# Turning the projections of a one-layer decoder round: activations stationary, 512 weight columns moving

## The chip, the cores and the metric

The kernel runs on one NeuronCore of a Trainium2 chip. The metric is the device time of one execution in microseconds, the median of several runs. A NeuronCore has a matrix engine (TensorE, "PE" in the profile; its weight loads are "PEld"), a vector engine (DVE), a scalar engine (ACT), GpSimd (POOL) and a queue engine that issues most DMAs (SP). A matrix product loads a stationary operand of 128 x 128 into the array and then streams a moving operand of up to 512 columns through it; the result goes into a PSUM bank of 512 floats per partition.

## The reference

One layer of a decoder trunk for 256 tokens of width 2048, in float32. Every `@` below is a projection with float32 weights:

```python
def swiglu(h, w_gate, w_up, w_down):
    return (jax.nn.silu(h @ w_gate) * (h @ w_up)) @ w_down      # d_ff = 5632
...
h = rms_norm(x, ffn1_norm[l])
x = x + 0.5 * swiglu(h, ffn1_w_gate[l], ffn1_w_up[l], ffn1_w_down[l])
h = rms_norm(x, mix_norm[l])
z = h @ w_in[l]
b_g, c_g, u, q_nsa, kv_nsa, g_nsa, q_mem, g_merge = jnp.split(z, split_at, axis=-1)
y_conv = short_conv_mixer(b_g, c_g, u, conv_w[l])
y_nsa = nsa_attention(q_nsa, kv_nsa, g_nsa, ...)
y_mem = memory_cross_attention(q_mem, rms_norm(mem, mem_norm[l]), w_mem_kv[l], ...)
ys = jnp.stack([y_conv, y_nsa, y_mem], axis=2)
yb = jnp.einsum('bsnc,ncd->bsnd', ys, w_branch[l])
merged = jnp.einsum('bsnd,bsnd->bsd', jax.nn.sigmoid(g_merge...), yb)
x = x + merged @ w_o[l]
x = x + 0.5 * swiglu(rms_norm(x, ffn2_norm[l]), ...)
```

## The kernel before, in words

The weights are cut into tiles of 128 x 128. There are 6736 of them in the projections: 256 for the memory's keys and values (`w_mem`), 2112 in each feed-forward network (`w_ffn1`, `w_ffn2`), 2256 between them (`w_mix`). They are stored in HBM in the order of their use and come in chunks of eight (512 KB) through `Stream.fetch`: one DMA, an ACT copy that rounds the chunk to the short float format fp32r (`whi`), and a DVE subtraction that gives the rest (`wlo`). Each activation is likewise held as two parts, high and low, and a product is the sum of three: high times high, low times high and high times low. Four buffers each of `wraw`, `whi` and `wlo` let ACT and DVE run ahead of PE.

Activations lie feature-major: 128 features on the partitions, 256 tokens along the row. `proj` takes a group of two weight tiles columns at a time and walks over the 16 slices of the inner dimension. For each weight tile it issues two matrix products with the weight tile stationary: `whi` against 512 columns (the high and the low part of the 256 tokens side by side, L232) and `wlo` against the 256 columns of the high part (L233). Such a couple is called a pair below; 768 columns stream in it. The two halves of a bank then have to be added: `evac` copies one half with ACT (L243) and adds the other with DVE (L244). The per-token factor of the RMS norm is applied by a DVE multiplication with a row `rb` that holds it for all partitions.

The work of the attention is written as generators. `proj` calls `tick` at a few places of a group, which takes each running generator one step on, so that scores, transposes and softmax stand between projection products on PE's queue, which runs in order. A scheduler then arranges the instructions of each engine. `compress` (attention's block compression, L546 and L553) builds its input by four small DMAs on POOL's queue, adds the position code on DVE (`Rk`, `Rv`) and runs 64 records of products 60 columns wide on PE (float32 products appear in the trace as two records each, transposes as one). Sums over features are products with a column of ones (L336, L347, 2 columns wide); transposes are products with the identity (L301, L357, L393, L507, L523 in the projections' service, L482, L637, L681 in the attention).

Of the kernel before, what the change touches and what calls it, by code (L numbers as in the profile page):

```python
# [10 lines left out]
F32 = mybir.dt.float32  # L11
# [6 lines left out]
P = 128  # L18
# [4 lines left out]
NQ = 4  # L23
HPQ = HID // NQ
# [8 lines left out]
def order(group, late):  # L33


    out = []
    if late == "k":
        n = len(group[0])
        out = [(j, kts[i], i == 0, i == n - 1) for i in range(n) for j, kts in enumerate(group)]
    elif late:  # L40
        for j, kts in enumerate(group):
            out += [(j, k, i == 0, False) for i, k in enumerate(kts[:len(kts) - late])]
        for j, kts in enumerate(group):
            rest = kts[len(kts) - late:]
            out += [(j, k, False, i == late - 1) for i, k in enumerate(rest)]
    else:
        for j, kts in enumerate(group):
            out += [(j, k, i == 0, i == len(kts) - 1) for i, k in enumerate(kts)]
    return out
# [4 lines left out]

def plan_mem():
    gs = [([("kv", f, ALLK) for f in range(4)], "k")]
    return gs + [([("kv", 2 * p, ALLK), ("kv", 2 * p + 1, ALLK)], 0) for p in range(2, 8)]


def plan_ffn():  # L60
    gs = []
    for q in range(NQ):
        for f in range(q * HPQ, (q + 1) * HPQ):
            gs.append(([("gate", f, ALLK), ("up", f, ALLK)], 2 if f == 0 else 0))
        ks = list(range(q * HPQ, (q + 1) * HPQ))
        for p in range(8):
            gs.append(([("down", 2 * p, ks), ("down", 2 * p + 1, ks)], 1 if p == 0 else 0))
    return gs


def plan_mix():
    gs = []
    for p in range(4):
        gs.append(([("qm", 2 * p, ALLK), ("qm", 2 * p + 1, ALLK)], 2 if p == 0 else 0))
    for i in range(0, 8, 2):
        gs.append(([("c", i, ALLK), ("u", i, ALLK)], 0))
        gs.append(([("c", i + 1, ALLK), ("u", i + 1, ALLK)], 0))
        gs.append(([("b", i, ALLK), ("b", i + 1, ALLK)], 0))
    for n in (0, 2, 4, None, 1, 3, 5):
        gs.append(([("ng", 0, ALLK)] if n is None else [("nkv", 2 * n, ALLK), ("nkv", 2 * n + 1, ALLK)], 0))  # L80
    for p in range(4):
        gs.append(([("nq", 2 * p, ALLK), ("nq", 2 * p + 1, ALLK)], 0))
    for br in (0, 2, 1):
        for d in range(KT):
            gs.append(([("gm%d" % br, d, ALLK), ("wb%d" % br, d, list(range(8)))], 0))
    for p in range(8):
        gs.append(([("wo", 2 * p, ALLK), ("wo", 2 * p + 1, ALLK)], 2 if p == 0 else 0))
    return gs
# [11 lines left out]
RAMP = (2, 2, 4)  # L100


def tiles_of(plan):
    return [(g[j][0], g[j][1], k) for g, late in plan for j, k, _, _ in order([m[2] for m in g], late)]
# [14 lines left out]
class Stream:  # L119
# [13 lines left out]

    def fetch(self):
# [11 lines left out]

class Trunk:
    def __init__(self, ctx, tc, a):
# [3 lines left out]
        self.xs = pool("xs", bufs=16)  # L152
        self.hp = pool("hp", bufs=16)
# [14 lines left out]
        z = self.tp.tile([P, 2, 512], BF16, name="zero", tag="t", bufs=3)  # L168
# [44 lines left out]
    def proj(self, stream, group, late, X, ticks=0, before=None, fold=False):  # L213


        nc = self.nc
        pw = self.psw.tile([P, 2, 512], F32, name="psw", tag="psw")
        pss = [pw[:, 0, :], pw[:, 1, :]]
        pss += [self.psa.tile([P, 512], F32, name="pso", tag=tag) for tag in ("sc", "o")[:max(0, len(group) - 2)]]
        seq = order([m[2] for m in group], late)  # L220
        at = [len(seq) * (n + 1) // ticks - 1 for n in range(ticks)]
        for n, (j, k, first, last) in enumerate(seq):
            if before:
                before(j, k)
            wh, wl = stream.next((group[j][0], group[j][1], k))
            x = X[j][k]
            ps = pss[j]
            if fold:
                for n2 in range(2):
                    nc.tensor.matmul(ps[:, :S], wh, x[:, n2, :], start=first and n2 == 0, stop=False)  # L230
            else:
# [4 lines left out]
        return [pw] + pss[2:]  # L236

    def evac(self, ps, t=None, part=slice(0, 2)):
        nc = self.nc
        ps = ps[0]  # L240
        if t is None:
            t = self.tp.tile([P, 2, S], F32, name="t", tag="t", bufs=3)
        nc.scalar.activation(t[:, part], ps[:, part, S:], AF.Copy)  # L243
        nc.vector.tensor_tensor(t[:, part], ps[:, part, :S], t[:, part], op=ALU.add)  # L244
        return t

    def split(self, src, pool=None, tag="h", scale=None):

        nc = self.nc
        h = (pool or self.hp).tile([P, 2, S], F32R, name=tag, tag=tag)  # L250
# [718 lines left out]
```

## Time and profile before

| | |
|---|---|
| time, median of 3 runs | 2486.95 us (2474.59 to 2487.94) |
| the profiled execution | 2491.16 us; its span on the core 2489.4 us |
| PE busy | 2476.5 us, 99% of the span, 14388 records |
| PEld (weight loads) | 2153.6 us, 14388: one for each product |
| DVE busy | 1591.1 us, 64% |
| ACT busy | 1206.1 us, 48% |
| POOL busy | 32.8 us, 1% |
| HBM traffic | 460 MB, mean 185 GB/s |

The span is the time from the first to the last instruction of the core. Products on PE are pipelined, so the length that the profile gives for one (397 ns for 512 columns) is longer than the time from its start to the start of the next; what a product costs in a row of products is read from the starts.

### The profile page before, as it was taken

Reading aid. Unit: us, or ns where it says so; the run is one execution under the profiler, and the core shown is the slowest. Engines: PE = TensorE matmul, PEld = TensorE weight load, DVE = VectorE, ACT = ScalarE, POOL = GpSimd, SP = SyncE. Lnnn points to the kernel's source line nnn. Section 1 sums busy time; section 2 is a strip of 40 time slices with the busy share of each in tenths; the row PEclk is TensorE's granted clock in tenths of the full one; section 3 lists DMA queues with packets and bytes.
Section 4 is the critical chain, followed back from the end, with each engine's and each line's share of the span. In section 5 each row is a group of like instructions: output and inputs, shape, how many; then the busy total and the mean of one; then the engine's idle time right before and its main releaser. Section 6 shows DMA issues by size and latency. Waiting matters only on the chain.

```text
span 2489.4 us, 36404 instructions
## 1 busy us (share of the span) xinstructions
PE 2476.5 (99%) x14388; PEld 2153.6 (87%) x14388; DVE 1591.1 (64%) x2190; ACT 1206.1 (48%) x1660; POOL 32.8 (1%) x42
## 2 busy tenths in 40 slices
PE   9999999999999999999999999999999999999999
PEld 7888888888888888888888888888888888888888
DVE  8666566566566766744677776666666666666665
ACT  7544444444445544433455554555544444444443
POOL 0000000000000000010000000000000000000000
PEclk9999999999999999999999999999999999999999
DMA  7666666665666754654545546666666666666665
GB/s 269 180 186 187 187 187 186 186 187 186 187 186 195 237 168 153 187 177 157 166 153 155 157 154 184 189 190 207 187 190 189 192 187 193 188 189 191 190 190 161
DMA packets 128348, 459.98 MB, mean 185 GB/s; under 512 B 14512, under 2 KB 15024, under 8 KB 127664
## 3 DMA queue, kind: packets, MB, share of 16 engines
q1 hardware_dynamic: 127152, 454.50, 58.9%
q0 software_dynamic: 1024, 3.14, 0.4%
q8 instruction: 113, 1.85, 0.3%
q14 instruction: 59, 0.48, 0.0%
HBM read 452.35 MB, written 4.19 MB: 183 GB/s over the span
## 4 chain that ended last, share of the span: by engine, by line
PE 98%; DMA 1%; DVE 0%; POOL 0%; ACT 0%; SPq 0%; issue 0%; DVEq 0%; ACTq 0%
PE psw L232 62%; PE psw L233 32%; PE phid L553 1%; PE sc L652 1%; PE pt L681 0%; PE on L688 0%; PE sc L464 0%; DMA wraw<-w_mem 0%; PE pso L232 0%; PE o L489 0%; DMA Ek<-t 0%; DMA Ev<-t 0%; PE psw L230 0%; PE pstat L347 0%; PE on L702 0%; PE scc L615 0%
## 5 line engine op out<-in xcount | busy, mean ns | idle before, releaser
L232 PE MATMUL psw<-xs,whi 128*128 128x512 f32 x4432 | 1567.0, 397 | 0.0
L144 DVE TENSOR_TENSOR wlo<-wraw,whi 128x1024 fp32r<-128x1024 f32 (+1 forms) x844 | 1031.4, 1223 | 766.9 <-ACT whi L143 764.9
L143 ACT ACTIVATE whi<-wraw 128x1024 fp32r<-128x1024 f32 (+1 forms) x844 | 892.2, 1057 | 1043.2 <-PE psw L232 654.5
L233 PE MATMUL psw<-xs,wlo 128*128 128x256 f32 x4432 | 1245.8, 281 | 0.0
L232 PEld LDWEIGHTS psw<-xs,whi 128*128 128x128 f32 x4432 | 834.0, 188 | 199.3 <-issue 5.2
L233 PEld LDWEIGHTS psw<-xs,wlo 128*128 128x128 f32 x4432 | 840.1, 190 | 0.1
L232 PE MATMUL psw<-h,whi 128*128 128x512 f32 x2122 | 747.8, 396 | 3.0 <-ACT whi L143 3.0
L233 PE MATMUL psw<-h,wlo 128*128 128x256 f32 x2144 | 601.8, 281 | 0.0
L232 PEld LDWEIGHTS psw<-h,whi 128*128 128x128 f32 x2122 | 398.3, 188 | 95.9 <-ACT whi L143 4.1
L233 PEld LDWEIGHTS psw<-h,wlo 128*128 128x128 f32 x2144 | 405.6, 189 | 0.7 <-DVE wlo L144 0.6
L244 DVE TENSOR_TENSOR t<-psw,t 128x512 f32<-128x512 f32 x233 | 159.1, 683 | 8.9 <-ACT t L243 8.8
L243 ACT ACTIVATE t<-psw 128x512 f32<-128x512 f32 x233 | 135.7, 582 | 27.3 <-PE psw L233 26.9
L252 ACT ACTIVATE h<-s 128x256 fp32r<-128x256 f32 x88 | 36.9, 419 | 114.1 <-DVE s L371 114.1
L253 DVE TENSOR_TENSOR h<-s,h 128x256 fp32r<-128x256 f32 x88 | 37.4, 425 | 42.2 <-ACT h L252 42.2
L368 DVE TENSOR_TENSOR t<-t,rb 128x512 f32<-128x512 f32 x88 | 60.9, 692 | 3.1
L232 PE MATMUL psw<-yn,whi 128*128 128x512 f32 x128 | 45.7, 395 | 0.0
L378 DVE SCALAR_TENSOR_TENSOR x<-t,x 128x512 f32<-128x512 f32 x63 | 43.6, 692 | 2.2
L667 ACT ACTIVATE L<-L,nb 128x128 f32<-128x128 f32 x64 | 28.6, 447 | 32.2 <-DVE nb L665 32.2
L371 DVE TENSOR_TENSOR s<-s,t 128x256 f32<-128x256 f32 x88 | 36.9, 419 | 1.0 <-ACT s L370 1.0
L233 PE MATMUL psw<-yn,wlo 128*128 128x256 f32 x128 | 36.0, 282 | 0.0
L370 ACT ACTIVATE s<-t 128x256 f32<-128x256 f32 x88 | 35.3, 402 | 0.0
L232 PEld LDWEIGHTS psw<-yn,whi 128*128 128x128 f32 x128 | 24.1, 188 | 5.7
(185 smaller groups left out, 742.8 us busy)
## 6 DMA issues: line engine op xcount, KB each, us to landing
wraw<-w_ffn SPq DMA_DIRECT2D x528, 512.0 KB, 3.6
wraw<-w_mix SPq DMA_DIRECT2D x282, 512.0 KB, 3.6
wraw<-w_mem SPq DMA_DIRECT2D x31, 512.0 KB, 4.7
xin<-memT SPq DMA_DIRECT2D x8, 256.0 KB, 5.1
x<-xT SPq DMA_DIRECT2D x8, 256.0 KB, 5.5
xspill<-x POOLq DMA_DIRECT2D x8, 256.0 KB, 3.4
xin<-xspill SPq DMA_DIRECT2D x8, 256.0 KB, 3.5
w<-w1k SPq DMA_DIRECT2D x2, 1024.0 KB, 6.2
```

The source lines that it names most:

```text
L143: nc.scalar.activation(self.wh[:, :w], raw[:, :w], AF.Copy)
L144: nc.vector.tensor_tensor(self.wl[:, :w], raw[:, :w], self.wh[:, :w].bitcast(F32), op=ALU.subtract)
L232: nc.tensor.matmul(ps, wh, x.rearrange("p a n -> p (a n)"), start=first, stop=False)
L233: nc.tensor.matmul(ps[:, :S], wl, x[:, 0, :], start=False, stop=last)
L243: nc.scalar.activation(t[:, part], ps[:, part, S:], AF.Copy)
L244: nc.vector.tensor_tensor(t[:, part], ps[:, part, :S], t[:, part], op=ALU.add)
L252: nc.scalar.activation(h[:, 0, :], src, AF.Copy)
L253: nc.vector.tensor_tensor(h[:, 1, :], src, h[:, 0, :].bitcast(F32), op=ALU.subtract)
L368: nc.vector.tensor_tensor(t, t, self.both(rb), op=ALU.mult)
L370: nc.scalar.activation(s, t[:, 0, :], AF.Silu)
L371: nc.vector.tensor_tensor(s, s, t[:, 1, :], op=ALU.mult)
L378: nc.vector.scalar_tensor_tensor(xp[pr][:, part], t[:, part], 0.5, xp[pr][:, part], op0=ALU.mult, op1=ALU.add)
```

## The change

For every projection but the three of the convolution (c, u, b: 384 tiles) the roles are exchanged. A 128-token slice of an activation part is stationary and 512 weight columns move. `proj_tokens` handles a block of 512 output columns for both token halves (`tt`): for each inner slice and token half three products of 512 columns, high x `whi`, high x `wlo`, low x `whi` (L258, L259, L260). Four weight tiles, which were four pairs of products (8 products, 3072 columns), are six products (3072 columns). All three sum into the same bank, so nothing is added afterwards; results lie token-major, 128 tokens on the partitions, and the norm's factor is a per-partition scale of the evacuating instruction. The next operand has to be feature-major again: `turn` makes it with four PE transposes into a bank of PSUM, and `split` makes high and low parts from there. Feed-forward stages run in thirds of the hidden width instead of quarters. Sums of squares are ACT accumulations instead of products with ones. `compress` builds its input by PE transposes and copies instead of DMAs, and its weights `w1` are loaded two at a time, earlier. One block is 304 columns wide and one 256 (`width`). The input x is read once more, token-major; the spill and the output are token-major.

```diff
-    def proj(self, stream, group, late, X, ticks=0, before=None, fold=False):
...
-            ps = pss[j]
...
-                nc.tensor.matmul(ps, wh, x.rearrange("p a n -> p (a n)"), start=first, stop=False)
-            nc.tensor.matmul(ps[:, :S], wl, x[:, 0, :], start=False, stop=last)
...
+    def proj_tokens(self, stream, group, turns, X, ticks=0, before=None, width=512):
...
+        for i0 in range(0, n, 2):
...
+            for tt in range(2):
+                for i, (wh, wl) in zip((i0, i0 + 1), ws):
+                    hi, lo = [X[ks[i]][:, n2, tt * P:(tt + 1) * P] for n2 in range(2)]
+                    wh, wl = wh[:, :width], wl[:, :width]
+                    nc.tensor.matmul(ps[:, tt, :width], hi, wh, start=i == 0, stop=False)
+                    nc.tensor.matmul(ps[:, tt, :width], hi, wl, start=False, stop=False)
+                    nc.tensor.matmul(ps[:, tt, :width], lo, wh, start=False, stop=i == n - 1)
+            for i in (i0, i0 + 1):
+                if i in at:
+                    self.tick()
...
+    def turn(self, x, col, to, step=None):
+        pt = self.psa.tile([P, 2, S], F32, name="pxt", tag="pt", bufs=2)
+        for j in range(2):
+            for tt in range(2):
+                nc.tensor.transpose(pt[:, j, tt * P:(tt + 1) * P], x[:, tt, col + j * P:col + (j + 1) * P], self.ident)
+        to(pt)
...
+    def hidden(self, t, out):
+        yield
+        for p in range(2):
+            h = self.parts()
+            self.turn(t, 2 * p * P, lambda pt: self.split(pt, h))
+            out += [h[:, 0], h[:, 1]]
...
-                t = self.evac(self.proj(stream, *next(plan), [Xs, Xs], ticks if f == 0 else 0))
-                nc.vector.tensor_tensor(t, t, self.both(rb), op=ALU.mult)
...
+                ps = self.proj_tokens(stream, *next(plan), Xs, ticks)
+                s = self.tp.tile([P, 2, 512], F32, name="s", tag="sl")
+                for tt in range(2):
+                    nc.scalar.activation(s[:, tt], ps[:, tt], AF.Silu, scale=r[:, tt:tt + 1])
+                ps = self.proj_tokens(stream, *next(plan), Xs, ticks)
+                t = self.room()
+                for tt in range(2):
+                    nc.vector.scalar_tensor_tensor(t[:, tt], ps[:, tt], r[:, tt:tt + 1], s[:, tt], op0=ALU.mult, op1=ALU.mult)
+                self.spawn(self.hidden(t, out))
...
-        for g in range(2):
-            nc.gpsimd.dma_start(Ev[0:64, :, g, :], t[64 * g:64 * g + 64, :, :])
-            nc.gpsimd.dma_start(Ev[64:128, :, g, 0:S - 1], t[64 * g:64 * g + 64, :, 1:S])
...
+                    nc.tensor.transpose(pt[:, n, tt * P:(tt + 1) * P],
+                                        t[:, tt, 2 * h + n].rearrange("p c d -> p (c d)"), self.ident)
```

In the order of the instructions, PE in the memory stage before: pairs of a 512- and a 256-column product, and four transposes of the values for a group behind (`ptok`; `h` is the normed memory, `psw` the bank, `par` holds the identity).

```order
L233 MATMUL psw<-h,wlo 128x256
L232 MATMUL psw<-h,whi 128x512
L233 MATMUL psw<-h,wlo 128x256
L357 MATMUL ptok<-par,t 128x128 x4
L232 MATMUL psw<-h,whi 128x512
L233 MATMUL psw<-h,wlo 128x256
```

In the feed-forward networks such pairs follow each other with nothing between them. PE there now, in the block behind the first gate and up blocks: the eight transposes of `tok` (gate times up) stand behind 24 products.

```order
L260 MATMUL pst<-whi,xs 128x512
L258 MATMUL pst<-whi,xs 128x512
L259 MATMUL pst<-wlo,xs 128x512
L260 MATMUL pst<-whi,xs 128x512
L295 MATMUL pxt<-par,tok 128x128 x8
L258 MATMUL pst<-whi,xs 128x512
```

What moved: every product has 512 columns, three stand where the step had pairs, and transposes now stand in the networks too.

ACT in the first network before (`t` is the evacuation of a group of four chunks, `s` silu, `h` the hidden part):

```order
L143 ACTIVATE whi<-wraw 128x1024 x3
L243 ACTIVATE t<-psw 128x512
L143 ACTIVATE whi<-wraw 128x1024
L370 ACTIVATE s<-t 128x256
L252 ACTIVATE h<-s 128x256
```

ACT there now (`s` is silu of a gate block; eight chunks make a block):

```order
L144 ACTIVATE whi<-wraw 128x1024 x11
L282 ACTIVATE h<-pxt 128x2x256 x2
L144 ACTIVATE whi<-wraw 128x1024 x5
L441 ACTIVATE s<-pst,rtok 128x512 x2
L144 ACTIVATE whi<-wraw 128x1024 x11
```

What moved: an evacuation comes once in eight chunks instead of once in four. Counted from the start of the program, three chunks of the following block stand ahead of each.

PE at the first `compress` before (`phid` is its product, `w_9649` a weight buffer):

```order
L233 MATMUL psw<-xs,wlo 128x256
L232 MATMUL psw<-xs,whi 128x512
L233 MATMUL psw<-xs,wlo 128x256
L553 MATMUL phid<-Rk,w_9649 128x60 x16
L232 MATMUL psw<-xs,whi 128x512
```

PE there now, where its input is transposed into `pE`; the first sixteen of `phid` follow 22 products behind the last row.

```order
L260 MATMUL pst<-whi,xs 128x512
L627 MATMUL pE<-par,kvc 128x128 x2
L258 MATMUL pst<-whi,xs 128x512
L259 MATMUL pst<-wlo,xs 128x512
L627 MATMUL pE<-par,kvc 128x128 x6
```

What moved: the compressing products keep their number, and what they wait for is made by PE, ACT and DVE instead of by DMAs.

## Rows read from the trace of the kernel before

**Rows 1.** The page: span, and busy time by engine.
```profile
span 2489.4 us, 36404 instructions
PE 2476.5 (99%) x14388; PEld 2153.6 (87%) x14388; DVE 1591.1 (64%) x2190; ACT 1206.1 (48%) x1660; POOL 32.8 (1%) x42
```

**Rows 2.** The page: the chain that ended last, shares by line.
```profile
PE psw L232 62%; PE psw L233 32%; PE phid L553 1%; PE sc L652 1%; PE pt L681 0%; PE on L688 0%; PE sc L464 0%; DMA wraw<-w_mem 0%; PE pso L232 0%; PE o L489 0%; DMA Ek<-t 0%; DMA Ev<-t 0%; PE psw L230 0%; PE pstat L347 0%; PE on L702 0%; PE scc L615 0%
```

**Rows 3.** Stretches: PE, PEld, DVE, ACT, POOL busy (records); granted clock; DMA.
```profile
100.00:850.00 750.00, 750.00 (x4250) 650.60 (x4249) 466.00 (x527) 358.62 (x453) 4.01 (x7) 1.00 0.61 190
...
1537.00:1750.00 213.00, 213.00 (x1225) 186.81 (x1224) 145.65 (x191) 111.89 (x153) 0.00 (x0) 1.00 0.63 194
1750.00:2470.00 720.00, 720.00 (x4155) 634.44 (x4154) 449.17 (x502) 342.50 (x427) 0.70 (x1) 1.00 0.62 191
```

**Rows 4.** PE in order of time, first feed-forward network: start, length, instruction.
```profile
300.00 0.40 PE L232 MATMUL psw<-xs,whi 128*128 128x512 f32 x1
300.24 0.28 PE L233 MATMUL psw<-xs,wlo 128*128 128x256 f32 x1
300.36 0.40 PE L232 MATMUL psw<-xs,whi 128*128 128x512 f32 x1
```

**Rows 5.** PE in order of time, memory stage: three 512-column products running.
```profile
18.91 0.39 PE L232 MATMUL psw<-h,whi 128*128 128x512 f32 x1
19.14 0.62 PE L232 MATMUL pso<-h,whi 128*128 128x512 f32 x2
19.60 0.28 PE L233 MATMUL psw<-h,wlo 128*128 128x256 f32 x1
```

**Rows 6.** PE in order of time, the last group: 256-column products alone.
```profile
2477.41 0.40 PE L230 MATMUL psw<-h,whi 128*128 128x256 f32 x2
2477.65 0.28 PE L233 MATMUL psw<-h,wlo 128*128 128x256 f32 x1
2477.77 0.40 PE L230 MATMUL psw<-h,whi 128*128 128x256 f32 x2
```

**Rows 7.** PE in order of time near the start, at half the clock.
```profile
12.24 1.05 PE L232 MATMUL pso<-h,whi 128*128 128x512 f32 x2
13.09 0.42 PE L233 MATMUL psw<-h,wlo 128*128 128x256 f32 x1
```

**Rows 8.** PE in order of time, six transposes between projection products.
```profile
1228.68 0.82 PE L681 MATMUL pt<-par,L 128*128 128x128 f32 x6
1229.26 0.48 PE L232 MATMUL psw<-xs,whi 128*128 128x512 f32 x1
1229.57 0.28 PE L233 MATMUL psw<-xs,wlo 128*128 128x256 f32 x1
```

**Rows 9.** PE in order of time, eight records of products with ones.
```profile
1104.85 0.40 PE L232 MATMUL psw<-xs,whi 128*128 128x512 f32 x1
1105.09 0.95 PE L347 MATMUL pstat<-par,sq 128*128 128x2 f32 x8
...
1106.10 0.39 PE L232 MATMUL psw<-xs,whi 128*128 128x512 f32 x1
```

**Rows 10.** Groups by line and shape on PE: count, busy us, mean ns, idle before.
```profile
L681 PE MATMUL pt<-par,L 128*128 128x128 f32 x96 | 15.8, 277 | 0.0
...
L347 PE MATMUL pstat<-par,sq 128*128 128x2 f32 x48 | 5.8, 242 | 0.0
```

**Rows 11.** Waits of PE: who waited for whom, us in total, times, longest.
```profile
PE phid L553 <- DVE Rk L546: 2.6, 1, 2.6
PE phid L553 <- DVE Rv L546: 1.7, 1, 1.7
```

**Rows 12.** Three stretches of the attention, columns as in Rows 3.
```profile
1076.00:1088.00 12.00, 12.00 (x54) 11.09 (x54) 3.37 (x5) 1.69 (x2) 0.00 (x0) 0.57 0.51 176
1134.00:1142.00 8.00, 8.00 (x38) 7.47 (x38) 3.38 (x4) 0.00 (x0) 0.00 (x0) 0.57 0.46 156
1202.00:1207.00 5.00, 5.00 (x25) 4.31 (x24) 4.03 (x18) 0.58 (x3) 0.70 (x1) 0.66 0.19 46
```

More of the change, by code (lines that the diff above doesn't have):

```diff
@@ L30, with order @@
 OFF_B, OFF_C, OFF_U, OFF_Q, OFF_KV, OFF_G, OFF_QM, OFF_GM = 0, 1024, 2048, 3072, 4096, 5632, 5680, 6704
[L33 to L49, printed above, removed]
+def order(group, turns):
+    n = len(group[0])
+    if turns:
+        return [(j, kts[i], i == 0, i == n - 1) for i in range(n) for j, kts in enumerate(group)]
+    return [(j, k, i == 0, i == n - 1) for j, kts in enumerate(group) for i, k in enumerate(kts)]
@@ L83, in plan_mix @@
+    gs += [four("nq", c) for c in range(2)]
     for br in (0, 2, 1):
[L84 to L87, printed above, removed]
+        for c in range(4):
+            gs += [four("gm%d" % br, c), four("wb%d" % br, c, list(range(8)))]
+    gs += [four("wo", c) for c in range(4)]
     return gs
@@ L132, in next, with wide @@
         return self.wh[:, s], self.wl[:, s]
+    def wide(self, group, k):
+        for n, (key, f, _) in enumerate(group):
+            wh, wl = self.next((key, f, k))
+            if n == 0:
+                at = (self.i - 1 - self.at) * P
+        s = slice(at, at + len(group) * P)
+        return self.wh[:, s], self.wl[:, s]
     def fetch(self):
@@ L247, in split @@
-    def split(self, src, pool=None, tag="h", scale=None):
+        assert turns
+        ps = self.psw.tile([P, 2, 512], F32, name="pst", tag="psw")
+        ks = group[0][2]
+        n = len(ks)
+        at = [n * (i + 1) // ticks - 1 for i in range(ticks)]
+        for i0 in range(0, n, 2):
+            ws = []
+            for i in (i0, i0 + 1):
+                if before:
+                    before(ks[i])
+                ws.append(stream.wide(group, ks[i]))
+            for tt in range(2):
[5 more added lines that the diff above has]
+                    nc.tensor.matmul(ps[:, tt, :width], lo, wh, start=False, stop=i == n - 1)
+            for i in (i0, i0 + 1):
+                if i in at:
+                    self.tick()
@@ L362, in ffn @@
+    def ffn(self, stream, Xs, r, x, finish, ticks=4):
         nc = self.nc
         plan = iter(plan_ffn())
[L364 to L381 removed]
@@ L488, in mem_head @@
             for mt in range(2):
-                nc.tensor.matmul(o[:, j, :], vm[h][:, mt, j, :], T[:, mt, :], start=mt == 0, stop=mt == 1)
-        for j in range(2):
-            out[2 * h + j] = self.split(o[:, j, :])
-    def nsa_key(self, t, r, gain, out):
-        nc = self.nc
-        sq = self.squares(t)
+                nc.tensor.matmul(o[:, j, :], vm[h][:, mt, j * P:(j + 1) * P], T[:, mt, :], start=mt == 0, stop=mt == 1)
+        y = self.parts()
+        self.split(o, y)
+        out[2 * h], out[2 * h + 1] = y[:, 0], y[:, 1]
@@ L831, in run, with merge_parts @@
                 self.nsa_pair(j, Q, CQ, kv, vcz, ptc, G, Yn)
-        queries()
-        queries()
-        merged = [mgp.tile([P, S], F32, name="mg%d" % d) for d in range(KT)]
+        self.spawn(self.nsa_queries(block(), r, CQ[1], Q[2:4]))
+        merged = mgp.tile([P, 2, D_MODEL], F32, name="merged")
         Mg = []
+        def merge_parts(c):
+            yield
+            for p in range(2):
+                h = self.parts()
+                self.turn(merged, 512 * c + 2 * p * P, lambda pt: self.split(pt, h, scale=0.5))
+                Mg.extend([h[:, 0], h[:, 1]])
         for bi, Y in enumerate((Yc, Ym, Yn)):
```

579 lines of the change are left out of this document (307 added, 272 removed).

## The prediction

> **What bounds the kernel now.** Read the page first: PE is busy for 2476.5 of 2489.4 us, while DVE and ACT are at 64% and 48% [rows 1]. The chain that ended last says the same of order: 94% of the span is the two lines of the projection pair [rows 2]. So nothing that DVE, ACT or the DMAs save is a gain by itself; only PE's own sequence counts. Next the stretches: between 100 and 850 us, which hold nothing but the first feed-forward network, PE takes 750 us for 4250 records, 176.5 ns a record or 352.9 ns a pair; between 1750 and 2470 us it is 720 us for 4155, 346.6 ns a pair; between 1537 and 1750 us, 347.8 ns [rows 3]. At the full clock of 2.4 GHz, which these stretches were granted, a pair's 768 columns alone would be 320 ns. The question is what makes the other 27 to 33 ns, and whether six products of 512 columns pay it six times or eight.
>
> **The columns' price.** The timeline gives the parts. Where 256-column products run alone, three start in 0.36 us: 120 ns each, where 256 columns need 106.7 [rows 6]. So a product pays about 13 ns over its columns. Three 512-column products in a row start at 18.91 and end with the start of the next at 19.60: 230 ns each, 17 over the columns' 213.3 [rows 5]. From the faster pair, 346.6 less 120 leaves 226.6 ns; from the slower, 352.9 less 120 leaves 232.9. In the first network a 512 before a 256 takes 240 ns and that 256 takes 120 [rows 4], so neighbours share the overhead in more than one way. At half the clock two 512-column products took 0.85 us, 425 ns each [rows 7]: half of that, 212.5, has no overhead in it and is the lower bound. The upper bound is 240.
>
> The added product has a row of nearly its own form in the three of rows 5 (512 columns, another 512 behind, a new stationary operand each), so the value lies near 230; the fixed overhead of rows 6 and the faster pair say 226.7. I take 228.5 ns. No row shows which of the two rates of rows 3 a uniform stream falls into, and that is the largest doubt.
>
> **The sum.** All counts of products are from the code.
>
> Removed: 6352 of 6736 pairs (the 384 of the convolution stay). Of these 3600 lie before 1537 us, at 352.9 ns 1270.4 us; 640 (the last branch and w_o) at 347.8 ns, 222.6 us; 2112 of the second network at 346.6 ns, 732.0 us. Together 2225.0 us.
>
> Added: 1568 steps of four tiles, 9408 products of 512 columns at 228.5 ns, 2149.7 us; 96 of 256 columns at 120 ns, 11.5 us; 96 of 304 columns, 120 and 48 columns more at (230 - 120)/256 ns, about 141 ns, 13.5 us. Together 2174.7 us. The gain so far is 50.3 us, and it hangs on one number: each ns of the 512-column price is 9.4 us.
>
> Transposes added, all on PE: 176 for the hidden layers (8 for each of 22 blocks), 64 for two norms, 32 for merged, 56 for queries and keys, 16 in compress, 344 in all. Rows 8 price them: from the first of six to the 256-column product behind the next 512 is 0.89 us; less 0.23 for that 512, 110 ns each [rows 8]. That is 37.8 us lost. The profile gives 277 ns as the length of one [rows 10], but six of them start within 0.58 us, so that length is latency, not cost.
>
> The Trainium skill ("TensorE: Matmul & The Clock Gate", section "Part 4: PE-mode transpose") puts a transpose in a kernel at about 275 ns and says that it doesn't engage the full clock. The trace has the same 277 ns, as a length; by starts it is 110, and 344 x 275 would be 94.6 us instead of 37.8.
>
> Products removed: 48 transposes at 110 ns (24 of the values, 8 and 8 of key scales, 2 of gates, 6 of the rows rb), 5.3 us; of products with ones 92 records (48 of L347 [rows 10], 32 of L336, 12 of the norms). Eight of those stretch a pair by 1.25 - 0.35 us, 112 ns each [rows 9], so 10.3 us. Together 15.6 us back.
>
> Waits: PE stands 2.6 and 1.7 us before the compressing products [rows 11], which wait for four small DMAs and an addition. Now transposes and two copies make that input, so 4.3 us go. If ACT and DVE, which also split weights, are late instead, all of it stays.
>
> Clock: three stretches of 12, 8 and 5 us near those products were granted 0.57, 0.57 and 0.66 of the clock [rows 12]. With two levels, 1.2 and 2.4 GHz, that is the lower one for 10.3, 6.9 and 3.4 us; half of these 20.6 us, 10.3, is what it cost. Ahead of the first two stood the waits of rows 11 and then narrow products; the waits go, the narrow products stay. I count half, 5 us (bounds 0 and 10.3).
>
> Costed at nothing: the evacuations. Before, ACT copies and DVE adds half a bank for each pair group; now one instruction for each token half reads the bank and the additions go. They lie beside PE either way: a block is 96 products, 22 us, two banks alternate, and ACT has three chunks (8 us of PE's work) rounded ahead when an evacuation makes it wait. DVE, at 466 of 750 us [rows 3], loses more than it gains. The hidden transposes stand 24 products, 5.5 us, behind the block's end, and need two DVE instructions by then. Without that cover each of 43 groups of eight would wait; at 1 us each that is 43 us. The weights' stream stays at one chunk for 2.7 us. The extra reading of x (2 MB) falls in the memory stage; chunks prefetched four deep cover it, and at the 190 GB/s of rows 3 it would cost 11 us without. Start and end: the first chunk has four tiles instead of two, and the last store is 256 KB; I charge 2 us.
>
> Sum: 50.3 - 37.8 + 15.6 + 4.3 + 5 - 2 = 35.4 us. The span goes from 2489.4 to 2454.0, the profiled time from 2491.2 to 2455.8; the profiled execution was 4.2 us over the median, so I forecast a median of 2451.5 us, 1.4% faster.
>
> **The rivals.**
>
> *The slow rate (ends slower).* In the first network a 512-column product takes between 232.9 ns (worked out above) and 240 [rows 4], 236.5 in the middle. If it costs that whatever stands next to it, the steps take 2225.0 us: 75.3 us more, 2526.8 us. For it: the slower rate held for all of 100 to 850 us [rows 3], so a stream can stay in it. Against it: three such products in a row took 230 [rows 5]. It decides from 232.3 ns on, where the sum is zero.
>
> *No overhead.* If a weight load hides under any 512-column product and only the short ones paid, the price nears the bound of rows 7: at 212.5, 150.5 us less, 2301. For it: a load is one per product and its recorded length (650.6 us for 4249, 153 ns of union each [rows 3]) fits under 213. Against it: rows 5 again, where a 512 stands before a 512.
>
> The Trainium skill's rule (same page, section "Back-to-back issue gap": columns/2.4 plus 2.5 ns) would be 215.8 ns, by it the time would be about 2332 us. The trace disagrees at 230.
>
> *Transposes cost their length.* At 277 ns, 57 us more: 2509. For it: the added ones read fresh DVE results and write banks that must be emptied, and eight come at once on two banks. Against: rows 8, in the same kind of place.
>
> *New waits.* If each group of eight waits 1 us, the time is 2494, no change. For it: PE runs in order, so one late operand holds all. Against: the 5.5 us above.
>
> **How the numbers follow.** The forecast case (226.7 to 231 ns, transposes at 110, few waits) gets 0.67, with its own range 2435 to 2475; the slow rate 0.13; no overhead 0.08; transposes at length 0.05; new waits 0.07. About 0.5% (12.4 us) is what a measurement here can tell from no change. The forecast case passes it up to 230.9 ns, which takes 0.02 to 0.03 off; with the case without overhead, faster has 0.72. Between 230.9 and 233.6 ns or with new waits the time is within 0.5%: 0.13. Slower: 0.15. The range leaves out the case without overhead and the slow rate's upper part, under 0.2 together: 2410 (224 ns) to 2510 us.
>
> **What would show it.** In the profile after: 512-column products starting 0.23 us apart in the networks; transposes in runs of eight at 0.11 us; PE still at 98 to 99%, DVE near 45 to 50%; no idle time named before `pxt` or `pst`; the wait at `phid` gone; fewer stretches at half clock. The prediction is wrong if the starts are 0.22 or 0.24 us apart, if PE idles at block ends behind ACT, or if the transposes' groups take over 1 us each.

## The result, and the profile after

The changed kernel takes 2442.81 us (median of 4 runs, 2441.52 to 2443.42) against 2480.77 us of the kernel before in the same session (4 runs, 2469.14 to 2487.94): ratio 0.9851 [0.9805, 0.9896], 1.5% faster. The forecast was 2451.5 us. The profiled execution took 2441.52 us, its span is 2439.7 us; that of before was 2489.4 [rows 1], so the spans differ by 49.7 us, where the sum of the prediction had 35.4. Between the medians the gain is 38.0 us. Two of the four runs of before took 2469.1 and 2474.6 us and the other two 2487.0 and 2487.9, so its median lies where no run does, and the profile of before is of a longer execution; the repeats of the kernel before, further below, come back to this.

The page after, span and busy time by engine, and the chain that ended last by line:

```profile
span 2439.7 us, 29544 instructions
PE 2426.0 (99%) x11466; PEld 2008.7 (82%) x11466; DVE 1325.1 (54%) x1602; ACT 1097.2 (45%) x1387; POOL 25.8 (1%) x24
...
PE pst L258 29%; PE pst L259 29%; PE pst L260 29%; PE psw L234 4%; PE psw L235 2%; PE pxt L295 1%; PE phid L641 1%; PE sc L740 1%; PE pt L769 0%; ACT whi L144 0%; PE on L776 0%; PE sc L544 0%; PE o L570 0%; DMA xin<-memT 0%; POOL hs L398 0%
```

PE is still busy for all but 13.7 us of the span; before it was all but 12.9 [rows 1]. The chain is the same one too: 87% lies in the three lines of the turned step, where the two lines of the pair had 94% [rows 2]. DVE lost 266 us of work and ACT 109, and neither shows in the span by itself.

The stretches that answer to [rows 3] (the two networks; columns as there) and, in a second view, the transposes of `turn` alone in these two stretches:

```profile
90.00:840.00 750.00, 750.00 (x3366) 621.90 (x3365) 379.62 (x358) 323.25 (x348) 3.60 (x5) 1.00 0.63 193
...
1700.00:2430.00 730.00, 730.00 (x3271) 605.50 (x3270) 367.04 (x337) 306.62 (x316) 0.72 (x1) 1.00 0.61 190
```
```profile
90.00:840.00 750.00, 14.50 (x112) 1.00 0.63 193
1700.00:2430.00 730.00, 12.41 (x96) 1.00 0.61 190
```

PE in order of time in the first network, at a group of transposes and in a stretch of products alone (start, length, instruction):

```profile
150.16 1.04 PE L295 MATMUL pxt<-par,tok 128*128 128x128 f32 x8
150.95 0.47 PE L258 MATMUL pst<-whi,xs 128*128 128x512 f32 x1
151.26 0.39 PE L259 MATMUL pst<-wlo,xs 128*128 128x512 f32 x1
...
300.05 0.39 PE L258 MATMUL pst<-whi,h 128*128 128x512 f32 x1
300.28 0.39 PE L259 MATMUL pst<-wlo,h 128*128 128x512 f32 x1
...
301.41 0.39 PE L258 MATMUL pst<-whi,h 128*128 128x512 f32 x1
```

Six products start between 300.05 and 301.41, 226.7 ns each. Eight transposes and the product behind them take 1.10 us from 150.16 to 151.26; less 0.23 for that product, a transpose is 109 ns. The two prices make up the whole stretch: 3254 products at 226.7 ns are 737.7 us and 112 transposes at 109 ns are 12.2, together 749.9 of 750.

What is left of PE's waits (who waited for whom, us in total, times, longest), and the chain just before the longest of them:

```profile
PE pxt L295 <- DVE tok L585: 2.9, 1, 2.9
PE pst L259 <- DVE wlo L145: 2.4, 4, 0.8
PE pst L258 <- ACT whi L144: 2.0, 2, 1.1
```
```profile
1084.50 3.83 POOL hs L398
...
1088.35 0.17 DVE ckn L399
...
1088.55 0.70 DVE Ev L630
...
1089.28 0.70 DVE tok L585
...
1090.12 0.45 PE pxt L295
```

The waits at `phid` [rows 11] are gone. A new one of 2.9 us stands at a group of transposes of the keys: DVE works in order, stood behind a POOL instruction of 3.8 us, and made `tok` only afterwards. Behind it came the only stretch at the lower clock level that holds products, 3.4 us long.

Where the 49.7 us were gained can be read from the starts of the stages. The first products of the first network, of the part between the networks and of the second network, before and then after:

```profile
105.69 0.40 PE L232 MATMUL psw<-xs,whi 128*128 128x512 f32 x1
...
852.26 0.40 PE L232 MATMUL psw<-xs,whi 128*128 128x512 f32 x1
...
1751.72 0.39 PE L232 MATMUL psw<-xs,whi 128*128 128x512 f32 x1
```
```profile
101.19 0.39 PE L258 MATMUL pst<-whi,xs 128*128 128x512 f32 x1
...
832.19 0.39 PE L258 MATMUL pst<-whi,xs 128*128 128x512 f32 x1
...
1706.33 0.39 PE L258 MATMUL pst<-whi,xs 128*128 128x512 f32 x1
```

So 4.5 us come from the start and the memory stage, 15.6 from the first network, 25.3 from the part between and 4.3 from the second network with the end.

### The profile page after: what moved, and what is told of

The parts are those of the page before. It is cut to its first block, busy times and chain, and to the rows that moved or that the text cites. A ratio compares the mean times of both kernels' runs of the same rounds, so it can differ in the third digit from the quotient of the medians.

```text
span 2439.7 us, 29544 instructions
## 1 busy us (share of the span) xinstructions
PE 2426.0 (99%) x11466; PEld 2008.7 (82%) x11466; DVE 1325.1 (54%) x1602; ACT 1097.2 (45%) x1387; POOL 25.8 (1%) x24
## 4 chain that ended last, share of the span: by engine, by line
PE 98%; ACT 1%; DVE 0%; DMA 0%; issue 0%; POOL 0%; SPq 0%; DVEq 0%; ACTq 0%
PE pst L258 29%; PE pst L259 29%; PE pst L260 29%; PE psw L234 4%; PE psw L235 2%; PE pxt L295 1%; PE phid L641 1%; PE sc L740 1%; PE pt L769 0%; ACT whi L144 0%; PE on L776 0%; PE sc L544 0%; PE o L570 0%; DMA xin<-memT 0%; POOL hs L398 0%
## 5 line engine op out<-in xcount | busy, mean ns | idle before, releaser
L258 PE MATMUL pst<-whi,xs 128*128 128x512 f32 (+2 forms) x2048 | 796.4, 389 | 0.0
L259 PE MATMUL pst<-wlo,xs 128*128 128x512 f32 (+2 forms) x2048 | 791.8, 387 | 0.0
L260 PE MATMUL pst<-whi,xs 128*128 128x512 f32 (+2 forms) x2048 | 791.7, 387 | 0.0
L258 PEld LDWEIGHTS pst<-whi,xs 128*128 128x128 f32 x2048 | 385.2, 188 | 79.2 <-issue 3.2
L260 PEld LDWEIGHTS pst<-whi,xs 128*128 128x128 f32 x2048 | 384.8, 188 | 77.8
L259 PEld LDWEIGHTS pst<-wlo,xs 128*128 128x128 f32 x2048 | 385.0, 188 | 75.8
L258 PE MATMUL pst<-whi,h 128*128 128x512 f32 x1088 | 426.4, 392 | 2.1 <-ACT whi L144 2.0
L259 PE MATMUL pst<-wlo,h 128*128 128x512 f32 x1088 | 424.2, 390 | 2.4 <-DVE wlo L145 2.4
L260 PE MATMUL pst<-whi,h 128*128 128x512 f32 x1088 | 423.7, 389 | 0.0
L258 PEld LDWEIGHTS pst<-whi,h 128*128 128x128 f32 x1088 | 204.3, 188 | 46.8 <-ACT whi L144 3.1
L259 PEld LDWEIGHTS pst<-wlo,h 128*128 128x128 f32 x1088 | 204.3, 188 | 45.5 <-DVE wlo L145 4.0
L260 PEld LDWEIGHTS pst<-whi,h 128*128 128x128 f32 x1088 | 204.2, 188 | 42.6
L234 PE MATMUL psw<-xs,whi 128*128 128x512 f32 x384 | 135.0, 397 | 0.0
L235 PE MATMUL psw<-xs,wlo 128*128 128x256 f32 x384 | 106.9, 278 | 0.0
L234 PEld LDWEIGHTS psw<-xs,whi 128*128 128x128 f32 x384 | 72.0, 187 | 16.5
L235 PEld LDWEIGHTS psw<-xs,wlo 128*128 128x128 f32 x384 | 72.3, 188 | 0.2
L453 DVE SCALAR_TENSOR_TENSOR x<-pst,x 128x512 f32<-128x512 f32 x48 | 30.9, 686 | 17.6 <-PE pst L260 17.6
```

Of the source, the lines that this page charges most:

```text
L258: nc.tensor.matmul(ps[:, tt, :width], hi, wh, start=i == 0, stop=False)
L259: nc.tensor.matmul(ps[:, tt, :width], hi, wl, start=False, stop=False)
L260: nc.tensor.matmul(ps[:, tt, :width], lo, wh, start=False, stop=i == n - 1)
L453: nc.vector.scalar_tensor_tensor(x[:, tt, cs], ps[:, tt], 0.5, x[:, tt, cs], op0=ALU.mult, op1=ALU.add)
```

## The experiments

The kernel before scatters far more (2467.5 to 2503.1 us over three sessions with medians 2486.9, 2484.0 and 2475.8) than the one after and its variants, which repeat within 2 to 10 us. So variants of the kernel after are set against its 2442.81 us, and their ratios against the before of their own session are given beside. Theories, for short: *overhead* (a product costs its columns plus a fixed part, so fewer products are the gain), against *columns alone*, *relief of DVE and ACT*, and *transposes hidden, or dear*.

**Twice as many products, same columns.** Every 512-column product of a turned step becomes two of 256.

```diff
-                    nc.tensor.matmul(ps[:, tt, :width], hi, wh, start=i == 0, stop=False)
...
+                    cuts = [slice(0, 256), slice(256, 512)] if width == 512 else [slice(0, width)]
+                    for q in cuts:
+                        nc.tensor.matmul(ps[:, tt, q], hi, wh[:, q], start=i == 0 and q.start == 0, stop=False)
...
```

> The changed kernel with every 512-column product issued as two of 256 columns (same operands, same sums, twice as many products and weight loads). Overhead per product (the theory: 13.3 ns over the columns at 2.4 GHz, so 226.7 ns for 512 and 120 ns for 256): 9408 x (240 - 226.7) = 125 us more than the changed kernel's 2443, so 2568 us. Price by columns alone (rival): 2443 us, no change. Starts of neighbouring products: 0.12 us by the theory, 0.113 by the rival.

2560.77 us (2559.74 to 2561.58), ratio 1.0317 [1.0258, 1.0376]: 118 us over the kernel after, 12.5 ns for each of the 9408 added products. PE in order of time:

```profile
300.15 0.40 PE L262 MATMUL pst<-wlo,h 128*128 128x256 f32 x2
300.39 0.40 PE L264 MATMUL pst<-whi,h 128*128 128x256 f32 x2
300.63 0.40 PE L260 MATMUL pst<-whi,h 128*128 128x256 f32 x2
```

Two products in 0.24 us, 120 ns each, as in [rows 6]. In the networks a uniform stream costs 226.7 ns for 512 columns and 120.0 for 256: both are the columns at 2.4 GHz plus 13.3 ns. Were columns alone paid for, nothing would have moved. The overhead is shown, and the turned form undoes itself when its products are made short.

**Every transpose of `turn` twice** (328 more; the second writes the same result).

```diff
-        for j in range(2):
-            for tt in range(2):
-                nc.tensor.transpose(pt[:, j, tt * P:(tt + 1) * P], x[:, tt, col + j * P:col + (j + 1) * P], self.ident)
+        for _ in range(2):
+            for j in range(2):
+                for tt in range(2):
+                    nc.tensor.transpose(pt[:, j, tt * P:(tt + 1) * P], x[:, tt, col + j * P:col + (j + 1) * P], self.ident)
```

> The changed kernel with each of the 328 transposes of turn() issued twice into the same place. Transposes at 110 ns on PE's path (the theory): 36 us more, 2479 us. Transposes at their recorded length of 277 ns: 91 us more, 2534 us. Transposes hidden in gaps that PE has anyway: 2443 us.

2477.78 us (2476.86 to 2479.27, 10 runs), ratio 0.997 [0.994, 1.0]: 35.0 us more, 107 ns a transpose. Sixteen of them in PE's order of time:

```profile
153.62 1.91 PE L296 MATMUL pxt<-par,tok 128*128 128x128 f32 x16
155.28 0.48 PE L258 MATMUL pst<-whi,xs 128*128 128x512 f32 x1
155.60 0.40 PE L259 MATMUL pst<-wlo,xs 128*128 128x512 f32 x1
```

1.98 us less 0.23 for the product, 109 ns each. They are on the path in full, neither hidden nor at the 272 ns that the trace gives as the length of one. With them doubled the gain of the change is almost gone.

**The old load on ACT and DVE.** One ACT copy and three DVE additions of 512 columns for each block, into a tile that nobody reads.

```diff
+        spare = self.sm.tile([P, 512], F32, name="spare", tag="spare")
+        nc.scalar.activation(spare[:, :width], ps[:, 0, :width], AF.Copy)
+        for tt in (1, 0, 1):
+            nc.vector.tensor_tensor(spare[:, :width], ps[:, tt, :width], spare[:, :width], op=ALU.add)
```

> The changed kernel with the work that left DVE and ACT put back: behind each block one ACT copy of half the bank pair and three DVE additions that read PSUM, into a scratch tile that nobody uses (some 150 blocks, about 0.6 us ACT and 2.1 us DVE each, 300 us of DVE in all). Theory (PE's own sequence alone counts): 2443 us within 4, and the starts of 512-column products stay 226.7 ns apart. Rival (part of the gain is that DVE and ACT disturb PE or its operands less): the time goes back towards 2481, at least 2455.

2450.76 us (2447.77 to 2454.85), ratio 0.9875 [0.9817, 0.9933]: 8 us more, beyond the 4 us of the theory and short of the 2455 us of the rival. The page, and the first network's stretch:

```profile
PE 2426.9 (99%) x11466; PEld 2009.8 (82%) x11466; DVE 1520.4 (62%) x1926; ACT 1153.1 (47%) x1495; POOL 22.3 (1%) x24
```
```profile
90.00:840.00 750.00, 750.00 (x3367) 622.21 (x3366) 443.14 (x458) 341.85 (x384) 2.89 (x4) 1.00 0.62 192
```

DVE carries 443 us in that stretch, nearly its old 466 [rows 3], and PE issues 3367 records instead of 3366. In the networks the rate of PE doesn't depend on DVE's load. What is lost lies elsewhere: PE idles 19.1 us of this execution's 2446.0 us span, 5.4 more than in the kernel after, the longest wait again at `phid` (2.9 us, for `Rv`). Half of the 5.4 is the experiment's own: behind the last product the added instructions stand ahead of the last addition and store, and the span ends 2.7 us later after that product than in the kernel after. The two longer runs (2453.5 and 2454.9 us) were granted 0.995 and 0.994 of the clock on the mean, the two shorter ones 0.998. So the smaller load is worth at most some us outside the networks, where attention's chains run through DVE, and none in them.

**The old roles, products in twos** (512, 512, 256, 256). If the mixed widths make the overhead, this halves the changes of width. Groups whose last slices come later keep the old order, here and in the next experiment.

```diff
+            for n in range(0, len(seq), 2):
...
+                for (j, k, first, last), (wh, wl) in zip(seq[n:n + 2], ws):
+                    nc.tensor.matmul(pss[j], wh, X[j][k].rearrange("p a n -> p (a n)"), start=first, stop=False)
+                for (j, k, first, last), (wh, wl) in zip(seq[n:n + 2], ws):
+                    nc.tensor.matmul(pss[j][:, :S], wl, X[j][k][:, 0, :], start=False, stop=last)
```

> The kernel before with the pairs of two weight tiles issued as 512, 512, 256, 256 columns instead of 512, 256, 512, 256; nothing else changed. Theory (a fixed overhead per product, and the slower of the two steady rates, 353 ns a pair, belongs to the strict alternation of 512 and 256): two tiles take 2 x 226.7 + 2 x 120 = 693 ns throughout, so the some 3600 to 4000 pairs that ran at 353 ns save 6.3 ns each, 23 to 25 us: about 2457 us, which would be over half of the changed kernel's gain without changing roles. Rival (the slower rate belongs to the places or the operands, not to the alternation): 2481 us, no change.

2478.1 us (2476.36 to 2479.98, 10 runs), ratio 0.9979 [0.9951, 1.0007]. The expectation failed: four pairs take 1.40 us (300.35 to 301.75 below), 350 ns each, a rate of its own between the two of before. The second network, which ran at 346.6 ns, now takes 348 as well, so it loses a part of what the first one gains.

```profile
300.35 0.63 PE L226 MATMUL psw<-xs,whi 128*128 128x512 f32 x2
300.81 0.40 PE L228 MATMUL psw<-xs,wlo 128*128 128x256 f32 x2
...
301.75 0.40 PE L226 MATMUL psw<-xs,whi 128*128 128x512 f32 x1
```

**The old roles, sixteen and sixteen.** All 512-column products of a tile column, then all its 256-column ones: a uniform stream without turning the roles.

```diff
+            for j, (name, f, kts) in enumerate(group):
+                ws = [stream.next((name, f, k)) for k in kts]
+                for i, (k, (wh, wl)) in enumerate(zip(kts, ws)):
+                    nc.tensor.matmul(pss[j], wh, X[j][k].rearrange("p a n -> p (a n)"), start=i == 0, stop=False)
+                for i, (k, (wh, wl)) in enumerate(zip(kts, ws)):
+                    nc.tensor.matmul(pss[j][:, :S], wl, X[j][k][:, 0, :], start=False, stop=i == len(kts) - 1)
```

> The kernel before with each tile column's products in two uniform runs: all 512-column products of its inner slices, then all 256-column ones; roles, counts and operands as before. Theory (uniform streams pay 13.3 ns over the columns, mixed ones a little more): 226.7 and 120 ns, 346.7 ns a pair with some ns at each change of width, 2464 to 2472 us, and a spread of a few us instead of 30. Rival (the rate has to do with 256-column products or with the weights being stationary): no better than 2478 us.

2466.82 us (2464.56 to 2470.32, 8 runs), ratio 0.9936 [0.9902, 0.9969]: faster than before, slower than the change.

```profile
307.25 3.82 PE L227 MATMUL psw<-xs,whi 128*128 128x512 f32 x16
310.91 2.08 PE L229 MATMUL psw<-xs,wlo 128*128 128x256 f32 x16
312.82 3.82 PE L227 MATMUL psw<-xs,whi 128*128 128x512 f32 x16
```

Sixteen pairs from 307.25 to 312.82 are 348 ns a pair, near 226.7 + 120.0 = 346.7: the 512-column products take 3.66 us, 228.8 ns each, and the 256-column ones 1.91 us, 119.4. The slow rate of the first network, 352.9, is gone. At 4.9 ns for each of the 3600 pairs that ran slow the gain would be 17.6 us. The second network takes 348 ns a pair here too, where it had 346.6, which costs some 3 us of that. The session shows 17.2 us between the medians, and the interval allows 8 to 24. So by the medians somewhat under half of what the change brought was to be had without changing any role. Against the lowest group of the runs of before (2467.5 to 2476.8 us, see the repeats below) some 5 us of it are left.

**Compression by DMA again.** The 16 transposes stay, but their result goes to its place through small DMAs on POOL's queue, as before.

```diff
-            nc.scalar.activation(E[0:64, 2 * h:2 * h + 2, :], pt[0:64], AF.Copy)
-            nc.vector.tensor_copy(E[64:128, 2 * h:2 * h + 2, 0:S - 1], pt[64:128, :, 1:S])
+            D = self.ep.tile([P, 2, S], F32, name="D" + kind, tag="D", bufs=2)
+            nc.scalar.activation(D, pt, AF.Copy)
+            for n in range(2):
+                nc.gpsimd.dma_start(E[0:64, 2 * h + n, :], D[0:64, n, :])
+                nc.gpsimd.dma_start(E[64:128, 2 * h + n, 0:S - 1], D[64:128, n, 1:S])
```

> The changed kernel with the input of compress moved into its place by DMAs on POOL's queue again (PE transposes, an ACT copy, then DMAs), the rest as changed. Theory: PE waits for the DMAs' landing at the compressing products as it did before (2.6 and 1.7 us there, up to twice that here since the transposes come first) and the clock falls once or twice more: 5 to 14 us more, 2448 to 2457 us. Rival (the waits before were covered by something else): 2443 us.

2455.86 us (2452.63 to 2461.88), ratio 0.9874 [0.983, 0.9917]: 13 us more. The profile is of the longest of the four runs, 20 us over the profile after. PE at the compressing products, here and then in the kernel after, and between them the granted clock (third number from the end) in two stretches here:

```profile
1066.37 13.62 PE L644 MATMUL phid<-Rk,w 128*128 128x60 f32 x64 [1.72 <-DVE Rk L639]
1109.64 12.61 PE L644 MATMUL phid<-Rv,w 128*128 128x60 f32 x64 [3.29 <-DVE Rv L639]
```
```profile
1066.00:1080.00 14.00, 13.63 (x65) 13.63 (x66) 2.32 (x3) 0.00 (x0) 0.00 (x0) 0.53 0.27 94
1109.00:1122.00 13.00, 12.36 (x64) 12.37 (x65) 2.60 (x3) 0.00 (x0) 0.00 (x0) 0.58 0.13 40
```
```profile
1059.05 3.68 PE L641 MATMUL phid<-Rk,w 128*128 128x60 f32 x32
1065.37 3.67 PE L641 MATMUL phid<-Rk,w 128*128 128x60 f32 x32
1094.64 7.25 PE L641 MATMUL phid<-Rv,w 128*128 128x60 f32 x64
```

The waits of 1.7 and 3.3 us come back with the DMAs, and 64 narrow products then run at 0.53 and 0.58 of the clock, nearly twice as long as the same 64 in the kernel after. So most of what the new `compress` saves is the clock behind the wait.

**The load's width.** Probe products are added between the memory stage and the first network, which only adds work (2465.83 us, one run): 24 each with 128, 64 and 32 stationary columns against 512 fp32r columns, and 24 in bf16.

```diff
+        for n, cols in (("probe128", 128), ("probe64", 64), ("probe32", 32), ("probebf", 0)):
...
+                    nc.tensor.matmul(o[:cols], M[i % 16][:, 0, :cols], st.wh[:, 512 * (i % 2):512 * (i % 2) + 512],
+                                     start=i == 0, stop=i == 23)
...
+                    nc.tensor.matmul(o, xb[:, :P], xb[:, P:], start=i == 0, stop=i == 23)
```

> The changed kernel with four runs of 24 products set between the memory stage and the first network, whose results nobody uses: 512 fp32r columns against a stationary operand of 128, 64 and 32 columns, and 512 bf16 columns against 128 bf16 columns. It is read from the starts, not from the time (21 us more). If the 13.3 ns over the columns belong to the product as such: 227 ns in all three fp32r runs. If they belong to the load of the stationary operand and grow with its columns: 227, 220 and 217 ns. If they belong to reading four-byte columns at full rate: bf16 at 214 to 216 and all fp32r at 227.

PE in order of time, then its busy time and that of its weight loads (second and third columns) in the four parts:

```profile
104.11 16.68 PE L533 MATMUL probe<-whi,h 128*128 128x512 f32 x72
120.63 5.35 PE L536 MATMUL probebf<-xb 128*128 128x512 bf16 x23
```
```profile
104.20:109.40 5.20, 5.20 (x25) 4.31 (x24) 0.00 (x0) 1.57 (x4) 0.00 (x0) 1.00 0.34 106
109.70:114.90 5.20, 5.20 (x25) 3.01 (x23) 0.00 (x0) 0.00 (x0) 0.00 (x0) 1.00 0.01 3
115.20:120.40 5.20, 5.20 (x25) 2.40 (x22) 0.00 (x0) 0.00 (x0) 0.00 (x0) 1.00 0.00 0
121.20:125.40 4.20, 4.20 (x21) 1.87 (x20) 1.23 (x1) 0.73 (x1) 0.00 (x0) 1.00 0.28 76
```

The loads shrink from 4.31 to 2.40 us in equal stretches, and the products don't come faster: 72 in 16.52 us are 229.4 ns each, by their starts 226.7, 230.0 and 231.7 ns for 128, 64 and 32 stationary columns (means). So the 13.3 ns aren't the load's length. In bf16 the mean is 215.8 ns (without one step in which a record is missing), 2.5 over the columns: the overhead goes with the four-byte operands. The bf16 products also repeat one stationary and one moving operand, where the others change theirs; that was not tested by itself. What in the engine makes the overhead stays open.

**The kernel before, three times more**, to see whether its scatter is a change between the two rates.

> The kernel before, profiled a second time, unchanged. Its times on this chip spread from 2471 to 2502 us. If the spread comes from how many of the pairs run at the slower of the two steady rates, the PE time of 100 to 850 us and of 1750 to 2470 us again gives 346.7 or 353 ns a pair and nothing between over long stretches, and the span follows the share: 2466 us if all ran at 346.7, 2489 at the share of the first profile, 2502 if nearly all ran at 353.

> The kernel before, profiled a third time, for its spread. If the spread comes from which stages run at the slower rate of 353 ns a pair, a run near 2471 shows the first network at 346.7 (2112 pairs, 13.5 us less), and one near 2502 shows the second network at 353 as well. If the rates stay with the stages as in both profiles so far, the spread has another cause.

> As the third: the kernel before, profiled a fourth time. A span away from 2485 to 2489 us with the same two rates in the two networks would put the spread down to something else than the pairs' rate.

They took 2486.93, 2484.82 and 2484.07 us. The first of them in the first network's stretch, to be set against [rows 3]:

```profile
100.00:850.00 750.00, 750.00 (x4251) 650.66 (x4250) 466.94 (x528) 357.97 (x452) 4.01 (x7) 1.00 0.59 189
```

All four profiles of this kernel show the same rate at the same place. Their spans differ in the attention (lower clock level for 20.5, 17.1, 10.2 and 6.8 us). But all four lie between 2484 and 2491 us, and the times of before fall into three groups with none between: of the 41 runs in the three sessions, 15 took 2467.5 to 2476.8 us, 22 took 2481.7 to 2491.4 and four 2496.4 to 2503.1. The granted clock doesn't make the groups: at a mean of 0.998 the times are 2469.5 and 2471.5, then 2482.7 to 2486.2, then 2496.4. The steps of 13 to 15 us are about what one network's 2112 pairs cost more at 352.9 than at 346.6 ns, 13.3 us. That fits what was expected of the spread, both networks at the quicker rate in the first group, one of them in the second, none in the third, and it speaks for a rate that changes from run to run. It is not shown: no run of the first or third group was profiled.

**An attempt to go further.** In the kernel after, the convolution's pairs stand as sixteen and sixteen, and the keys' transposes one tick later, so that they needn't wait.

```diff
+            for i, (k, (wh, wl)) in enumerate(zip(ks, ws)):
+                nc.tensor.matmul(ps, wh, X[k].rearrange("p a n -> p (a n)"), start=i == 0, stop=False)
+            for i, (k, (wh, wl)) in enumerate(zip(ks, ws)):
+                nc.tensor.matmul(ps[:, :S], wl, X[k][:, 0, :], start=False, stop=i == len(ks) - 1)
...
+        yield
```

> The changed kernel with two small edits: the convolution's 384 pairs in uniform runs (16 products of 512, then 16 of 256 columns), and the transposes of the attention's keys one tick later, where PE waited 2.9 us for DVE. By the prices shown so far: 384 x (351 - 347) = 1.5 us and 2.9 us less than the changed kernel, 2438 to 2440 us. If the waiting moves on to the next tick and the conv's runs only crowd the evacuation: 2443 us or a little more.

2450.48 us (2448.99 to 2452.08, 6 runs), ratio 0.9882 [0.9842, 0.9921]: 8 us slower than the kernel after, though its PE idles only 11.8 us. PE at the second compression:

```profile
1093.78 13.91 PE L642 MATMUL phid<-Rv,w 128*128 128x60 f32 x64 [0.61 <-DVE Rv L637]
```

The waits at the keys fell from 2.9 to 1.5 us, but a short one of 0.6 us now stands right before the 64 narrow products, and they take 13.9 us instead of 7.25. The clock had already fallen ahead of that wait: of the three 304-column products before it, the last two start 0.25 us apart, where such products start 0.14 us apart at the full clock. The stretch at the lower level is 20.5 us instead of 3.4: half of the difference is 8.6 us, as much as the whole loss. No version tried beats the kernel after.

## Why the prediction held, step by step

**What bounds it**: right. PE's sequence sets the time before and after, and the old load on DVE and ACT doesn't change PE's rate in the networks. (The stretch of 100 to 850 us isn't the first network alone: until 105.7 us it holds the end of the memory stage. The rate of 353 ns isn't touched by that.)

**The columns' price**: the mechanism was right, the term was mis-sized. The prediction took 228.5 ns between the fixed-overhead value of 226.7 and the 230 of [rows 5]; a uniform stream in the networks gives 226.7. Over 9408 products that is 16.9 us more gain: 67.2 instead of 50.3. The doubt which rate a uniform stream falls into was justified: 226.7 and 120.0 are the prices in the networks, after and in e1, and their sum of 346.7 is the faster rate of the mixed pairs, while the slower one of the first network pays 6.2 ns on top. But the 192 products with `yn` stationary run at 233.3 ns without a break, six in 1.40 us:

```profile
1502.68 0.40 PE L258 MATMUL pst<-whi,yn 128*128 128x512 f32 x1
...
1504.08 0.40 PE L258 MATMUL pst<-whi,yn 128*128 128x512 f32 x1
```

That is the slow rate of the first rival, for 2% of the products. What decides between the rates stays open, and the rows of before could not tell that most of the turned products would fall into the quicker one. Against the fast rate a turned step of four tiles saves 4 x 346.7 - 6 x 226.7 = 27 ns, two overheads and no more; against the slow one 51 ns.

**Transposes**: right, 107 ns (doubled) to 109 (by starts) against 110. The 344 cost 37 us. This is where an expected gain is given back: in the second network 2112 pairs at 346.6 were 732.0 us; 3168 products at 226.7 and 88 transposes at 109 are 727.8. Only 4 us are left there, while the first network, which ran at 352.9, gains 14 (745.3 against 718.2 and 13.1 for 120).

**Waits**: the step failed in part, and with it two signs that the prediction named: no idle time before `pxt` or `pst`, where 2.9 and 4.4 us stand, and DVE near 45 to 50%, which came to 54. The 4.3 us at `phid` did go, as said, but PE's idle time in the whole span is 13.7 us against 12.9: 2.9 us at the keys' transposes stand in its place, and waits for weight chunks went from 3.0 us (two, for `whi`) to 4.4 (six, for `whi` and `wlo`). The prediction looked for late operands behind ACT's and DVE's evacuations; the one that came was behind a POOL instruction in DVE's order.

**Clock**: 5 us were counted, half of the bound. One stretch of 3.4 us is left of 20.6, so between these two profiles 8.6 us came back. The profile of before was the one with the most: from the 17.1, 10.2 and 6.8 us of the other three, 6.8, 3.4 and 1.7 us would have come back, so half of the bound was a fair price and its size in one pair of profiles is chance. The compression by DMA together with its waits was priced at 9.3; putting the DMAs back costs 13.

**The sum again**, between the two spans: 67.2 - 37 + 15.6 - 0.8 (idle time) + 8.6 = 53.6, measured 49.7. A fourth stretch at the lower level, 3.4 us near the start of the profile of before (the one of [rows 7]), is missing in the prediction and in the profile after; with its 1.7 us the sum is 55.3. Of the 5.6 us too much about 4 lie between the networks: the same prices give some 29.5 us there (1872 pairs less, 120 transposes more, 9.6 us of small products less, clock and waits), and 25.3 were gained, while in the networks they come out to within 1 us. The `yn` products explain 1.3 of it. The 2 us charged for start and end, and the 15.6 us for removed small products, which no run here tested, are the other terms left.

**The rivals**: the slow rate (236.5 ns) for all products and no overhead (212.5) both fall with 226.7. Transposes at their length fall with the doubled ones. New waits came to a few us, not to 1 us for each of 43 groups. On the rule from the Trainium skill ("TensorE: Matmul & The Clock Gate", section "Back-to-back issue gap") that the prediction set against the trace: its 215.8 ns is met here by bf16 (215.8) and not by fp32r (226.7).

**The forecast**, 2451.5, was 8.7 us too slow. Of that, 6.2 us are the kernel before, whose median was 2486.95 us when the forecast was made and 2480.77 in the session of the result. The gain between the medians, 38.0 us, is near the 35.4 of the sum, but that is luck in part: the products gained more than was counted, the waits and the part between the networks less, and the median of before depends on how many of its runs fall into each group. Against the lowest of them the change would gain some 30 us, against the middle one some 45.

## What to carry to other kernels

Before turning a matrix product round, count both products and columns: where each product pays a fixed part (13.3 ns here) the gain is that part times the products saved, and the transposes that the turned result needs (109 ns each, all on the path of a bound PE) can take most of it back, 9.6 of 13.8 us in the second network. Look for the same gain in the order of the products first: grouping equal widths gave 17 us against the median of before with no other change. Look at the single times of a kernel and not only at their median, since it can lie between groups. And a wait of a microsecond or so ahead of a batch of narrow products costs several times its length when they then run at the lower clock.

## What the runs showed of the hardware that was not expected

- Alternating 512- and 256-column products run at one of several steady rates (346.6, 352.9, in twos and sixteens 348 to 350 ns a pair), the same at the same place in four profiles, all from one of three groups of run times. Uniform streams of 512 columns have several too: 226.7 ns in the networks, 233.3 with `yn`, 230.0 and 231.7 in two of the probes.
- The fixed part of a product is not shortened by a narrower weight load (231.7 ns with 32 stationary columns) and is 2.5 ns instead of 13.3 in bf16, there with operands that repeat.
- The same 64 products of 60 columns take 7.25 us at the full clock and 12.6 to 13.9 us at the lower level, and a wait of 0.6 us right ahead, with others of 1.3 and 0.4 us in the 4 us before it, went with the latter. In the kernel after the clock fell too, behind the wait of 2.9 us, but nine 304-column products without a wait stood between that stretch's last transposes and the narrow ones, the clock rose during them, and the narrow ones kept it.
